# Twenty-four stores of routing blocks issued from SyncE's DMA queue where ScalarE's queue issued them

## The chip, the cores and the metric

The kernel runs on one core of a Trainium2 chip. The core has five engines that run their own instruction streams: TensorE (PE in the profile), VectorE (DVE), ScalarE (ACT), GpSimd (POOL) and SyncE (SP). ACT and SP can each issue DMAs, each on a queue of its own; SP does nothing else here. Data lie in HBM, in the on-chip memory SBUF, and in PSUM, into which PE writes. The metric is the device time of one execution in microseconds (us), as the median of several runs; lower is better.

## What is computed

A two-layer trunk over 512 tokens of 1024 features: an mLSTM mixer in the first layer, stick-breaking attention in the second, and after each a PEER feed-forward block. Only the PEER block matters here. For every token and each of 8 heads it picks 16 of 16384 experts by two lists of 128 keys, and sums those experts:

```python
s_top, i_top = lax.top_k(s, PEER_TOPK)                       # per head, two lists of 128 keys
cand = s_top[:, :, 0, :, None] + s_top[:, :, 1, None, :]     # 16 x 16 pairs
g_top, pos = lax.top_k(cand, PEER_TOPK)
expert = jnp.take_along_axis(cand_idx, pos, axis=-1)
g = jax.nn.softmax(g_top, axis=-1)
u = jnp.take(peer_u, expert, axis=0)
act = jax.nn.gelu(jnp.einsum('thkd,td->thk', u, xb))
vv = jnp.take(peer_v, expert, axis=0)
out = jnp.einsum('thk,thkd->td', g * act, vv)
```

## The kernel before

For 384 of the 512 tokens the kernel does not gather: it computes all 16384 activations as 128 dense blocks (`ua` or `pp`, 24 matmuls of 128x384 each), multiplies them by a dense matrix of routing weights that is zero where an expert was not picked, and multiplies the product with `peer_v` (`y`). The other 128 tokens are gathered, by GpSimd, later on.

`peer(l)` runs once in each layer. The part that the change touches is its **routing stage**, in which two things are woven together on the same engines:

- The routing weights are made in 48 chunks of 8 tokens. VectorE writes one-hot rows `oA`, `oB` (L1021, L1022), GpSimd scales them to `oH` (L1024), VectorE and ScalarE make the low-order part `oL` (L1028, L1033), PE multiplies them into `gps` (L1041, L1042), and ScalarE copies `gps` out of PSUM into the block `stg` (L1044, twice in a chunk). After every fourth chunk a block of 32 tokens is full and is stored to HBM, to `Gd` (L1046): 12 stores in each layer, 24 in all. `stg` has two buffers, `gps` two.
- Between the chunks stand 64 of the dense activation blocks (`early_acts`). For each, SyncE loads 512 KB of `peer_u` into `wraw` (L915, three buffers), ScalarE casts it to `whi` (L917), VectorE takes the remainder `wlo` (L925), which frees `wraw`, PE makes 24 matmuls (L936), and ScalarE applies Gelu (L942 or L945). From the 17th block on the result is stored to HBM as `spd` (L946), from ScalarE's queue, 48 times in each layer.

The order on PE, VectorE and ScalarE is the order in which this code is written (`manual_schedule`); SyncE's is set by a scheduler. On ScalarE a store of `spd` is followed by the cast of the load that is used two blocks later:

```python
nc.scalar.dma_start(spd[a // 4][:, (a % 4) * ND:(a % 4 + 1) * ND], ga)   # L946
```

After the routing stage the next one begins with loads `gb` of the stored weights (L1134, SyncE's queue), which wait until all 12 stores of the layer have landed, and goes on with the matmuls `y` (L1177) and the other 64 activation blocks `pp` (L1125).

Of the kernel before, what the change touches and what calls it, by code (L numbers as in the profile page):

```python
# [49 lines left out]
def body(tc, nc, A, ctx):  # L50
# [803 lines left out]
    def peer(l):  # L854
        U, Vw, Ur, Vr = A["u"][l], A["v"][l], A["u_rows"][l], A["v"][l].rearrange("a p d -> (a p) d")
        Gd = dram.tile([NGRP, 128, GROW], F32, name=f"g{l}")
        keep = KEEP[l]
        with ExitStack() as st:
# [19 lines left out]
            with ExitStack() as s1:  # L878
# [156 lines left out]
                def place(s, c, stg, oB, oA, oH, oL, gl, o):  # L1035

                    for j in range(CHUNK // 4):
                        gps = pq.tile([128, 4, 128], F32, name="gps", bufs=2)
                        for i in range(4):
                            n = 4 * j + i  # L1040
                            PE.matmul(gps[:, i], oB[:, n], oH[:, n], start=True, stop=False)  # L1041
                            PE.matmul(gps[:, i], oB[:, n], oL[:, n], start=False, stop=True)  # L1042
                        k = c * CHUNK + 4 * j
                        S.activation(stg[:, :, k:k + 4], gps.rearrange("p t a -> p a t"), AF.Copy, scale=1.0 / GSCALE)  # L1044
                    if c == 32 // CHUNK - 1:
                        nc.scalar.dma_start(Gd[:, :, s * 128:(s + 1) * 128].rearrange("g p c -> p g c"),  # L1046
                                            stg.rearrange("p (g a) t -> p g (a t)", a=4))

                late = None
# [8 lines left out]
                for t in range(NGT, 4):  # L1058
                    gen = routed(t + 1) if t < 3 else gathered()
                    for sub in range(4):  # L1060
                        stg = gp.tile([128, 128, 32], F32, name="stg")
                        for c in range(32 // CHUNK):
                            ones_of = expand(t, sub * 32 + c * CHUNK)
                            advance(gen, RCHUNK)
                            sofar += 1
                            ran += share()
                            if late:
                                place(*late)
                            scale(*ones_of)
                            sofar += 1  # L1070
                            ran += share()
                            late = ((t - NGT) * 4 + sub, c, stg, *ones_of)
                    advance(gen, 1e9)
                place(*late)
                run(24 * NPRE)

# [221 lines left out]
```

## Time and profile before

| | |
|---|---|
| median of 3 runs | 3242.69 us (3240.5 to 3249.38) |
| the profiled execution | 3245.62 us |
| its span in the profile | 3243.9 us |
| routing stage, first store to last, layer 0 | 554.4 to 823.2 us |
| routing stage, first store to last, layer 1 | 2171.7 to 2436.0 us |
| DMA bytes of ScalarE's queue | 69.29 MB in 112944 packets |
| DMA bytes of SyncE's queue | 451.75 MB in 119680 packets |

Times in the trace are counted from the start of the span. An engine's name with a q behind it (ACTq, SPq) is its instruction sequencer, which issues DMAs; such an instruction counts as no work of the engine, but the engine's next instruction waits for it. A wait "A <- B" says that A stood idle until B's last instruction was done.

### The profile page before, as it was taken

The page shows a single profiled execution, that of the slowest core. Times are in us where ns is not written, and L with a number is a line of the kernel's source. Part 1 is how long each engine was busy: PE and PEld are TensorE (multiplying, and loading weights), DVE is VectorE, ACT ScalarE, POOL GpSimd, SP SyncE. Part 2 cuts the span into 40 slices and gives each one's busy share as a digit, 9 for nine tenths or more (in the row PEclk, how much of TensorE's full clock was granted, in tenths as well). Part 3 has the DMA queues.
Part 4 walks back from the last instruction along what each step waited for, and adds up shares of the span by engine and source line. Part 5 has one row for each costly group of instructions (what it writes and reads, how often), then busy time and mean ns, then how long its engine had stood idle before and what let it go on. Part 6 is the DMA issues. An engine that isn't in the chain of part 4 may idle for free. (4 is left out here: it accounts for less than half of the span.)

```text
span 3243.9 us, 45180 instructions
## 1 busy us (share of the span) xinstructions
PE 3127.5 (96%) x16168; PEld 2660.2 (82%) x16168; DVE 2440.9 (75%) x4501; ACT 1351.9 (42%) x2133; POOL 1497.3 (46%) x1592
## 2 busy tenths in 40 slices
PE   7998999999999999999989999999999999999999
PEld 5746789988888888888867657898988888888887
DVE  5745479777688788888883584897776888888887
ACT  5344335556433333333342553356663333333332
POOL 0433523887344444444453454248883444443443
PEclk9979999999999999999989899999999999999999
DMA  6733224676899899999854102246779998999997
GB/s 249 258 123 118 79 72 143 208 237 208 321 354 342 328 362 336 343 352 330 314 190 142 39 7 80 73 144 213 235 219 331 342 354 329 355 347 337 356 331 273
DMA packets 306578, 792.40 MB, mean 244 GB/s; under 512 B 24368, under 2 KB 135216, under 8 KB 306352
## 3 DMA queue, kind: packets, MB, share of 16 engines
q1 hardware_dynamic: 119680, 451.75, 39.1%
q0 software_dynamic: 73728, 268.47, 22.7%
q10 hardware_dynamic: 112944, 69.29, 7.3%
q8 instruction: 126, 2.06, 0.3%
q14 instruction: 100, 0.82, 0.1%
HBM read 718.12 MB, written 71.30 MB: 243 GB/s over the span
## 5 line engine op out<-in xcount | busy, mean ns | idle before, releaser
L103 ACT CAST whi<-wraw 128x1024 fp32r<-128x1024 f32 x481 | 501.2, 1049 | 676.2 <-PE y L1177 245.0
L1024 POOL TENSOR_SCALAR oH<-oA,gh 128x128 f16<-128x128 f16 x768 | 467.0, 630 | 249.4 <-DVE oA L1021 212.6
L104 DVE TENSOR_TENSOR wlo<-wraw,whi 128x1024 fp32r<-128x1024 f32 x393 | 477.7, 1223 | 135.1 <-ACT whi L103 133.5
L1095 POOL DMA_INDIRECT rows<-in_u_rows,pidx x256 | 337.5, 1318 | 472.5 <-DVE rows L1102 415.0
L1095 POOL DMA_INDIRECT rows<-in_v,pidx x256 | 326.5, 1276 | 447.8 <-DVE yt L1113 403.9
L1177 PE MATMUL y<-wlo,Wh 128*128 128x512 f32 x1536 | 480.7, 391 | 0.0
L1177 PE MATMUL y<-whi,Wl 128*128 128x512 f32 x1536 | 472.6, 390 | 0.0
L1177 PE MATMUL y<-whi,Wh 128*128 128x512 f32 x1536 | 443.9, 392 | 7.5 <-ACT Wh L103 7.5
L104 POOL TENSOR_TENSOR wlo<-wraw,whi 128x1024 fp32r<-128x1024 f32 x88 | 221.5, 2519 | 377.9 <-ACT whi L103 377.9
L936 PE MATMUL ua<-hh,wlo 128*128 128x384 f32 x1024 | 348.2, 340 | 2.9 <-DVE wlo L925 2.9
L936 PE MATMUL ua<-hh,whi 128*128 128x384 f32 x1024 | 347.4, 339 | 1.4 <-ACT sf L895 1.4
L936 PE MATMUL ua<-hl,whi 128*128 128x384 f32 x1024 | 346.8, 339 | 0.0
L1125 PE MATMUL pp<-hh,wlo 128*128 128x384 f32 x1024 | 343.7, 336 | 0.2
L1125 PE MATMUL pp<-hl,whi 128*128 128x384 f32 x1024 | 343.7, 336 | 0.0
L1125 PE MATMUL pp<-hh,whi 128*128 128x384 f32 x1024 | 343.2, 335 | 0.0
L1177 PEld LDWEIGHTS y<-whi,Wh 128*128 128x128 f32 x1536 | 287.6, 188 | 62.1 <-ACT Wh L103 9.0
L1177 PEld LDWEIGHTS y<-wlo,Wh 128*128 128x128 f32 x1536 | 289.2, 188 | 59.4
L1177 PEld LDWEIGHTS y<-whi,Wl 128*128 128x128 f32 x1536 | 288.2, 188 | 59.5
L1113 DVE SCALAR_TENSOR_TENSOR yt<-rows,uw,yt 128x1024 f32<-128x1024 f32 x254 | 327.0, 1288 | 8.9 <-DMA rows<-in_v,pidx 6.6
L1102 DVE SCALAR_TENSOR_TENSOR rows<-rows,htok 128x1024 f32<-128x1024 f32 x256 | 308.9, 1219 | 13.5 <-DMA rows<-in_u_rows,pidx 13.4
L119 PE MATMUL pp<-hh,whi 128*128 128x512 f32 x560 | 223.7, 407 | 14.1 <-ACT hh L234 7.2
L119 PE MATMUL pp<-hl,whi 128*128 128x512 f32 x560 | 224.9, 402 | 0.0
(320 smaller groups left out, 5629.9 us busy)
## 6 DMA issues: line engine op xcount, KB each, us to landing
wraw<-in_u SPq DMA_DIRECT2D x256, 512.0 KB
wraw<-in_v SPq DMA_DIRECT2D x256, 512.0 KB
g<-stg ACTq DMA_DIRECT2D x24, 2048.0 KB
gb<-g SPq DMA_DIRECT2D x64, 768.0 KB
araw<-in_ada_w SPq DMA_DIRECT2D x80, 512.0 KB
spd<-ga ACTq DMA_DIRECT2D x96, 192.0 KB
ga<-spd SPq DMA_DIRECT2D x24, 768.0 KB
wraw<-in_peer_q SPq DMA_DIRECT2D x32, 512.0 KB
```

What stands on the lines that cost most here:

```text
L103: S.copy(hi, src)
L104: eng.tensor_tensor(lo, src, hi.bitcast(F32), op=OP.subtract)
L119: PE.matmul(ps, a[:, ws], b[k], start=k == 0 and i == 0, stop=k == KD - 1 and i == 2)
L936: PE.matmul(ps, p[:, ws], q[k][:, T0:T], start=n == 0, stop=n == 3 * KD - 1)
L1024: G.tensor_scalar(oH[:, n], oA[:, n], gh[:, o + n:o + n + 1], 1.0, op0=OP.mult, op1=OP.mult)
L1095: tc.keep_in_program_order(G.indirect_dma_start(out=r, out_offset=None, in_=rows, in_offset=bass.IndirectOffsetOnAxis(ap=pidx[:, n:n + 1], ...
L1102: V.scalar_tensor_tensor(r, r, 1.0, htok, op0=OP.mult, op1=OP.mult, accum_out=uw[:, n:n + 1])
L1113: V.scalar_tensor_tensor(yt, r, uw[:, n:n + 1], yt, op0=OP.mult, op1=OP.add)
L1125: PE.matmul(ps[:, :ND], p[:, ws], q[k][:, T0:T], start=n == 0, stop=n == 3 * KD - 1)
L1177: PE.matmul(y[t][d], wa[:, ts], vb[:, d * 512:(d + 1) * 512], start=n == 0 and i == 0, stop=n == NA - 1 and i == 2)
```

## The change

One line: the store of a full routing block is issued from SyncE's queue. What it copies, and when its data are ready, stay as they were.

```diff
                     if c == 32 // CHUNK - 1:
-                        nc.scalar.dma_start(Gd[:, :, s * 128:(s + 1) * 128].rearrange("g p c -> p g c"),
+                        nc.sync.dma_start(Gd[:, :, s * 128:(s + 1) * 128].rearrange("g p c -> p g c"),
                                             stg.rearrange("p (g a) t -> p g (a t)", a=4))
```

The order on PE, VectorE and GpSimd is the same row for row. On ScalarE, layer 0, around the second store, this stood before (`stg` the block, `gps` the product in PSUM, `ga` a Gelu result):

```order
L1044 ACTIVATE stg<-gps 128x128x4 x2
L1046 DMA g_2427<-stg 128x32x128
L1033 ACTIVATE oL<-oA,gl 128x128 x3
L945 ACTIVATE ga<-ua 128x384
L946 DMA spd_4_2441<-ga 128x384
L917 CAST whi<-wraw 128x1024
```

and of a later store, as a piece of the difference:

```order
 L917 CAST whi<-wraw 128x1024
 L1044 ACTIVATE stg<-gps 128x128x4 x2
-L1046 DMA g_2427<-stg 128x32x128
 L1033 ACTIVATE oL<-oA,gl 128x128 x3
 L945 ACTIVATE ga<-ua 128x384
```

The store has left ScalarE's stream, and nothing else there has moved. On SyncE, layer 0, the whole routing stage and the first loads behind it stood like this before:

```order
L108 DMA wraw<-in_peer_q 128x1024 x10
L915 DMA wraw<-in_u 128x1024 x64
L108 DMA wraw<-in_u 128x1024 x3
L108 DMA wraw<-in_v 128x1024
L108 DMA wraw<-in_u 128x1024
L108 DMA wraw<-in_v 128x1024 x2
L1134 DMA gb<-g_2427 128x1536 x2
```

Now the stores stand among the loads. SyncE, layer 0, the last three of the twelve:

```order
L915 DMA wraw<-in_u 128x1024 x3
L1046 DMA g_2427<-stg 128x32x128
L915 DMA wraw<-in_u 128x1024 x5
L108 DMA wraw<-in_u 128x1024
L1046 DMA g_2427<-stg 128x32x128
L108 DMA wraw<-in_u 128x1024 x2
L108 DMA wraw<-in_v 128x1024
L108 DMA wraw<-in_u 128x1024
L108 DMA wraw<-in_v 128x1024
L1046 DMA g_2427<-stg 128x32x128
L108 DMA wraw<-in_v 128x1024
L1134 DMA gb<-g_2427 128x1536 x2
```

Ahead of the first store stand 20 loads of `peer_u`, and between one store and the next 3 to 6 loads; in layer 1 the same numbers return. Each load behind a store is issued after it.

## Rows read from the trace of the kernel before

**Rows 1.** The page: busy us, share of the span and instructions of each engine

```profile
PE 3127.5 (96%) x16168; PEld 2660.2 (82%) x16168; DVE 2440.9 (75%) x4501; ACT 1351.9 (42%) x2133; POOL 1497.3 (46%) x1592
```

**Rows 2.** DMA issues by line, layer 0: minimum/median/maximum ns, first and last start us

```profile
L946 ACTq DMA_DIRECT2D spd<-ga x48: 326/327/7011, 559.4 to 821.1; - x48
...
L1046 ACTq DMA_DIRECT2D g<-stg x12: 377/377/394, 554.4 to 823.2; - x12
...
L915 SPq DMA_DIRECT2D wraw<-in_u x49: 327/328/340, 530.0 to 790.3; - x49
```

**Rows 3.** ScalarE's longest wait, total us, times, longest; layer 0, then layer 1

```profile
ACT whi L917 <- issue: 49.6, 10, 7.1
...
ACT whi L917 <- issue: 47.9, 10, 6.6
```

**Rows 4.** Whom PE waited for, first to last store of layer 0: us, times, longest

```profile
PE gps L1041 <- ACT stg L1044: 6.3, 7, 1.5
PE gps L1042 <- ACT oL L1033: 5.2, 8, 1.1
```

**Rows 5.** The same of layer 1

```profile
PE gps L1042 <- ACT oL L1033: 5.5, 9, 1.1
PE gps L1041 <- ACT stg L1044: 3.6, 5, 1.1
```

**Rows 6.** The same, 2360 to 2370 us, where ScalarE changes its function table

```profile
PE gps L1042 <- ACT oL L1033: 1.1, 1, 1.1
PE gps L1041 <- ACT stg L1044: 1.1, 1, 1.1
```

**Rows 7.** The same behind the tenth stores: layer 0, then layer 1

```profile
PE gps L1041 <- ACT stg L1044: 0.9, 1, 0.9
...
PE gps L1042 <- ACT oL L1033: 0.5, 1, 0.5
...
PE gps L1041 <- ACT stg L1044: 0.6, 1, 0.6
```

**Rows 8.** In order of time (start, us, instruction [idle before]): layer 0's tenth store, SyncE's next loads

```profile
771.66 0.39 ACTq L1046 DMA_DIRECT2D g<-stg  x1
...
771.75 1.56 SPq L915 DMA_DIRECT2D wraw<-in_u  x2
...
773.50 7.01 ACTq L946 DMA_DIRECT2D spd<-ga  x1
780.55 1.05 ACT L917 CAST whi<-wraw 128x1024 fp32r<-128x1024 f32 x1 [7.08 <-issue]
...
784.23 1.05 ACT L917 CAST whi<-wraw 128x1024 fp32r<-128x1024 f32 x1 [0.40 <-ACT ga L945]
```

**Rows 9.** In order of time: a load on SyncE and its cast, no store near

```profile
2103.48 0.33 SPq L915 DMA_DIRECT2D wraw<-in_u  x1
...
2108.26 1.05 ACT L917 CAST whi<-wraw 128x1024 fp32r<-128x1024 f32 x1 [0.17 <-DMA wraw<-in_u]
```

**Rows 10.** In order of time: loads after layer 0's first store, casts behind stores one and two

```profile
557.38 1.57 SPq L915 DMA_DIRECT2D wraw<-in_u  x2
...
564.57 1.06 ACT L917 CAST whi<-wraw 128x1024 fp32r<-128x1024 f32 x1 [0.47 <-DMA wraw<-in_u]
567.41 1.09 ACT L1044 ACTIVATE stg<-gps 128x512 f32<-128x512 f32 x2 [1.79 <-PE gps L1042]
...
574.77 0.38 ACTq L1046 DMA_DIRECT2D g<-stg  x1
...
586.05 0.49 ACT L945 ACTIVATE ga<-ua 128x384 f32<-128x384 f32 x1 [0.84 <-PE ua L936]
```

**Rows 11.** The chain that ended last, in order of time: end of layer 1's routing stage

```profile
2436.05 11.73 DMA g<-stg
```

**Rows 12.** PE in order of time: two products that follow each other without a wait

```profile
2434.40 0.22 PE L1041 MATMUL gps<-oH,oB 128*128 128x128 f16 x1
2434.45 0.22 PE L1042 MATMUL gps<-oL,oB 128*128 128x128 f16 x1
```

## The prediction

> **What bounds the kernel now.** The page comes first: PE is busy for 96% of the span [rows 1]. So what can be won lies where PE has gaps, and the view to read next is that of the issues by line, on the queue that the change relieves. The store of `spd` at L946 takes 0.33 us to issue as a rule but up to 7.0 us [rows 2]. In order of time the long ones stand right behind a routing store: at 771.66 the store is issued, at 773.50 the next issue on the same queue begins and lasts 7.01 us, and the cast that follows in ScalarE's stream stands idle for 7.08 us [rows 8]. ScalarE loses 49.6 us in ten such waits in layer 0 and 47.9 us in ten in layer 1 [rows 3], 4.9 us each. The trace shows so much: an issue behind one of these stores (4096 runs of 512 bytes, by the code) is held up for 4 to 7 us.
>
> What matters is what PE loses by it. Between the first and the last store PE waits for ScalarE's `stg` copies and `oL` parts for 6.3 + 5.2 = 11.5 us in layer 0 and 5.5 + 3.6 = 9.1 us in layer 1 [rows 4, 5]: 20.6 us in 29 waits, against 97.5 us that ScalarE stands. Most of the stalls are covered, since ScalarE catches up before PE needs it.
>
> **What the change removes.** ScalarE's stream loses 24 issues of 0.377 us [rows 2] and, if the stall goes with the store, the twenty waits. Not all of PE's 20.6 us are owed to the stall. At four places ScalarE changes its function table for the `exp` of the routing; one of them costs PE 1.1 + 1.1 us [rows 6], the four 2.2, 2.2, 1.5 and 1.5, together 7.4 us in 8 waits. Behind each layer's first store, where no stall follows, PE waits 0.5 us once; that leaves 20.6 - 7.4 - 1.0 = 12.2 us in 19 waits. The two tenth stores hold 0.9 + 0.5 and 0.6 + 0.5 = 2.5 us of it in 4 waits [rows 7], which I expect to stay (next part): 9.7 us in 15 waits go. Each wait costs PE somewhat more than the view says: a product of `gps` shows 0.22 us but the next begins 0.05 us later [rows 12], so a break loses about 0.16 us besides. 15 x 0.16 = 2.4 us, and the term is 12.1 us.
>
> **What it adds.** SyncE's stream gets 24 issues; the store is then ahead of the loads on SyncE's queue. Three things can cost there.
>
> First, SyncE may wait for a full `stg` with loads behind it. By the order and the trace it hardly does: the load that now stands behind the store was issued later than the store already, as its buffer came free only then: 3.0 us later at the first store (554.4 and 557.38) [rows 2, 10], and 0.1 us at the tenth, the closest of layer 0 [rows 8]. I put this at nothing; who would wait is the cast of that load.
>
> Second, the issue of the next load is held up as that of `spd` is now, and its data come behind the store's. The trace has no load behind a store on one queue, so I bound its landing, counted from the store's issue. Below: in layer 0 a load issued at 557.38, 3.0 us after the first store but on the other queue, let its cast go at 564.57, 10.2 us after the store [rows 10]. Above: the store takes 11.7 us from its issue to the first instruction that waited for it [rows 11], and an undisturbed load takes 4.8 us from issue to cast [rows 9]: 16.5 us if the load began only when the store is done. Between them, as the issue comes free 5.7 to 8.9 us after the store (8.85 at the tenth, rows 8), the load would land 4.5 us later, at 10.2 to 13.3 us; I take 12, as `spd`'s held issue is the nearest row. When is it wanted? ScalarE casts two earlier loads first. Behind the second store the third cast follows a Gelu that starts 11.3 us after the store and itself waited for PE [rows 10], so removing the stall does not move it: it is wanted at 12.2 us, and I take this for ten stores of each layer, at no cost. At the first stores it is wanted at 10.2 us, 1.8 us too soon; ScalarE's next copy idles 1.79 us for PE there [rows 10], so most is covered: 0.5 us each, bounds 0 and 1.8. At the tenth store the load behind it is the second cast. Blocks follow each other every 5.4 us (49 loads in 260 us, rows 2), so without a stall that cast is wanted about 7.4 us after the store and gets its data at 12; now it stands at 784.23, 12.6 us after the store [rows 8]. A stall of ScalarE's queue is swapped for a wait for a load, with PE's 2.5 us unchanged.
>
> Third, the last store of each layer, on which the next stage waits, 11.7 us [rows 11]. It keeps its place in time; between 1 us sooner (no loads of the other queue between its packets) and 1 us later I take nothing.
>
> **The sum.** 12.1 - 2 x 0.5 = 11.1 us off the profiled execution's 3245.6 us gives 3234.5 us. That execution lies 2.9 us above the median of the runs shown, so the forecast is 3242.7 - 11.1 = 3231.6 us, 0.34% less. What a measurement of this kernel can tell from no change is about 0.3%, 9.7 us: the line stands at 3233.0 us, close by.
>
> **The rivals.** *No change: the loads hold ScalarE where its queue did.* If a load lands at the upper bound of 16.5 us, a cast wanted at 12.2 us waits 4.3 us at nearly every store, against 4.9 us now; PE gets back 0.6/4.9 of the 12.1 us, 1.5 us: 3241 us. For it speaks that the store and the load now share a queue; against it, that 10.2 us and the held issue bring the landing nearer to 12. The Trainium skill has another reason for the same outcome: "DMA: Bandwidth & Descriptors", section "Issuing engines are not separate DMA queues", says that DMAs of all issuing engines share the same 16 engines and that issuing from several saves only the sequencer's time, usually small beside the transfer. By that rule the sum would be nothing, 3242.7 us; the trace does not agree as far as the time of the issue goes, up to 7.0 us instead of 0.33 [rows 2].
>
> *Slower: ScalarE is held as before, and the loads come late besides.* This is so if an issue on one queue has to wait while the other queue's store is being issued. Then ScalarE loses its 4.9 us per store and up to 4.3 us more for the load; if PE's loss grows in proportion it nearly doubles, 12.2 us and 19 x 0.16 = 3.0 us: 15 us more, 3258 us. It is decided by one thing, whether `spd`'s issue stays long with the store on the other queue. The mirror image is in the trace: in layer 0 SyncE issued 49 loads while ScalarE's queue carried the stores, one at 557.38, 3.0 us after a store, and none took over 0.34 us [rows 2, 10]. That speaks clearly against it. [...]
>
> *Faster than forecast.* With ScalarE 5 us ahead the waits at the table changes and the tenth stores may shrink too. The most there is to win is all 29 waits: 20.6 + 29 x 0.16 = 25.2 us, 3217 us.
>
> **How the numbers follow.** My forecast, 0.57, with 0.44 below 3233.0 us and 0.13 above it, as the gain is close to the line and its terms are good to some 5 us; no change, 0.25; slower, 0.09, of which 0.01 would still be within 0.3%; faster than forecast, 0.09. So faster by over 0.3% has 0.44 + 0.09 = 0.53, within it 0.13 + 0.25 + 0.01 = 0.39, slower 0.08. The range goes from 3217 us, the most there is to win, to 3247 us, the no-change case with a load or two still later and the spread of the runs; it leaves out the slower rival and little else.
>
> **What would show it.** In the profile after, no issue at L946 should last over about 0.4 us, and the wait of `whi` for the queue should be gone; if it stays, the slower rival holds. Some load at L915 behind each store should take 4 to 8 us to issue. Casts at L917 should wait for `wraw` at the first and tenth stores, by 2 and 4 us; if they wait at nearly every store, it is the no-change case. PE's waits for `stg` and `oL` in the stage should fall from 20.6 us to about 11 us, and each layer's last store should come 5 to 6 us sooner after its first. A store that SyncE reaches well before `stg` is full, with loads waiting behind it, would make the prediction wrong in a way that I put at nothing.

## The result, and the profile after

The changed kernel takes 3199.87 us (median of 4 runs, 3193.14 to 3208.78), the kernel before beside it 3245.29 us: a ratio of 0.988, with a 95% interval of 0.985 to 0.991. The forecast was 3231.6 us with a range from 3217 to 3247 us. The direction was right; the gain is about four times as large as foretold, and the time lies below the range. The profiled execution takes 3194.85 us, its span is 3193.1 us, 50.8 us less than before.

Where those 50.8 us are, by the first and last store of each layer: at the first store of layer 0 the changed kernel is 1.5 us ahead (552.9 for 554.4), at the last 21.0 us (802.2 for 823.2), at the first of layer 1 34.4 us (2137.3 for 2171.7), at the last 49.2 us (2386.8 for 2436.0), at the end 50.8 us. So the two routing stages gave 19.5 and 14.8 us, 34.3 us in all, and the part between them 13.4 us. The stages are the change's doing; the part between is taken up below.

The page's first part, the counterpart of [rows 1], has PE at 97%: 32.8 us less busy for the same instructions.

```profile
PE 3094.7 (97%) x16168; PEld 2645.3 (83%) x16168; DVE 2437.3 (76%) x4501; ACT 1355.2 (42%) x2133; POOL 1510.2 (47%) x1592
```

The issues by line (minimum, median and maximum in ns; first and last start in us), both layers for L946 and for the stores, layer 0 for the loads at L915, the counterparts of [rows 2]:

```profile
L946 ACTq DMA_DIRECT2D spd<-ga x96: 326/326/336, 557.3 to 2384.7; - x96
...
L1046 SPq DMA_DIRECT2D g<-stg x24: 377/377/387, 552.9 to 2386.8; - x24
...
L915 SPq DMA_DIRECT2D wraw<-in_u x44: 327/328/4917, 555.8 to 774.1; - x44
```

The long issues have left `spd` and gone to the loads behind a store. SyncE now stands in front of each store until the block is full. Its waits in layer 0's stage (us, times, longest), and the eleventh store with the load behind it (start, us):

```profile
SPq L1046 <- ACT oL L1033: 31.9, 11, 4.5
...
SPq L1046 <- ACT stg L1044: 0.8, 1, 0.8
```

```profile
781.19 0.38 SPq L1046 DMA_DIRECT2D g<-stg  x1
781.83 6.75 SPq L108 DMA_DIRECT2D wraw<-in_u  x1
```

(The view names `oL`, the instruction behind the copy; each of these waits ended within 0.03 us of the end of the last copy into `stg`.) No load is late by these 32.7 us: in both layers the buffer of the load behind a store comes free only after the store is issued, 0.6 us after it at the closest, which is the eleventh.

The waits of layer 0's stage (us, times, longest), where [rows 3, 4] have `whi` standing 49.6 us for the queue and PE 11.5 us for `stg` and `oL`:

```profile
ACT stg L1044 <- PE gps L1042: 30.7, 30, 1.9
...
DVE wlo L925 <- ACT whi L917: 12.2, 7, 2.8
ACT whi L917 <- DMA wraw<-in_u: 7.7, 5, 3.5
...
PE gps L1041 <- POOL oH L1024: 2.7, 6, 0.8
ACT whi L103 <- DMA wraw<-in_u: 2.2, 1, 2.2
```

PE's matmuls wait for ScalarE nowhere; only its six short waits for GpSimd are left. ScalarE now waits for PE. Casts do wait for their loads, 7.7 + 2.2 us, but PE does not notice. Layer 1 reads the same, with 7.0 + 1.8 us for the casts and 2.1 us of PE for GpSimd.

Each stage in one row (length in us, busy us and instructions of PE, PEld, DVE, ACT and POOL, granted clock, DMA share, GB/s), first before, then after:

```profile
554.40:823.20 268.80, 253.96 (x1865) 240.78 (x1864) 207.64 (x432) 162.00 (x324) 210.40 (x342) 0.99 0.71 218
2171.70:2436.00 264.30, 252.50 (x1865) 239.26 (x1864) 207.51 (x432) 161.87 (x325) 214.78 (x342) 0.99 0.73 222
```

```profile
552.90:802.20 249.30, 246.20 (x1864) 236.88 (x1863) 207.04 (x432) 163.45 (x324) 219.36 (x342) 1.00 0.76 235
2137.30:2386.80 249.50, 246.97 (x1872) 238.00 (x1871) 206.87 (x432) 163.76 (x324) 219.53 (x342) 1.00 0.76 235
```

PE's idle time in the two stages (length less busy) was 14.8 + 11.8 = 26.6 us and is 3.1 + 2.5 = 5.6 us: 21.0 us, close to the 20.6 us of waits of [rows 4, 5]. Its busy time for the same work fell too, by 7.8 + 5.5 = 13.3 us. The gain of 34.3 us is these two numbers, and the second is one that the list of PE's waits does not have.

### The profile page after: what moved, and what is told of

Same layout as the page of the kernel before. It is cut to its first block, busy times and chain, and to the rows that moved or that the text cites. A ratio compares the mean times of both kernels' runs of the same rounds, so it can differ in the third digit from the quotient of the medians.

```text
span 3193.1 us, 45198 instructions
## 1 busy us (share of the span) xinstructions
PE 3094.7 (97%) x16168; PEld 2645.3 (83%) x16168; DVE 2437.3 (76%) x4501; ACT 1355.2 (42%) x2133; POOL 1510.2 (47%) x1592
## 5 line engine op out<-in xcount | busy, mean ns | idle before, releaser
L1024 POOL TENSOR_SCALAR oH<-oA,gh 128x128 f16<-128x128 f16 x768 | 480.7, 648 | 205.5 <-DVE oA L1021 200.5
```

The costliest lines, as they stand in the source:

```text
L1024: G.tensor_scalar(oH[:, n], oA[:, n], gh[:, o + n:o + n + 1], 1.0, op0=OP.mult, op1=OP.mult)
```

## The experiments

**What the theories were.** After the result the question was how PE can win more than ScalarE's late copies cost it. *Theory A:* a stall that lies ahead of a change of ScalarE's function table comes back round VectorE. The rows of ScalarE in the kernel before, behind layer 0's fourth store:

```profile
622.08 0.38 ACTq L1046 DMA_DIRECT2D g<-stg  x1
...
623.89 5.80 ACTq L946 DMA_DIRECT2D spd<-ga  x1
629.74 1.05 ACT L917 CAST whi<-wraw 128x1024 fp32r<-128x1024 f32 x1 [5.88 <-issue]
...
642.07 1.28 ACT L777 ACT_TABLE_LOAD   x1
646.76 0.31 ACT L777 ACTIVATE eg<-eg 128x128 f32<-128x128 f32 x1 [3.40 <-DVE eg L775]
647.09 1.28 ACT L945 ACT_TABLE_LOAD   x1
```

and VectorE's in the same stretch:

```profile
626.12 0.24 DVE L757 FIND_INDEX8 px<-gt,cd 128x8 uint32<-128x84 f32 x1
630.82 1.23 DVE L925 TENSOR_TENSOR wlo<-wraw,whi 128x1024 fp32r<-128x1024 f32 x1 [4.46 <-ACT whi L917]
...
646.44 0.28 DVE L775 TENSOR_TENSOR eg<-gt 128x128 f32<-128x128 f32 x1
```

The held issue delays the cast; VectorE, in order, stands 4.46 us for the cast at `wlo` (L925), and all its further work comes later, the input `eg` of the routing's `exp` among it (L775). ScalarE has caught up meanwhile, arrives at the `exp` (L777) too early, and stands again, 3.40 us, in front of a second table load. One stall has stopped ScalarE twice. After the change ScalarE finds its input ready:

```profile
638.62 1.28 ACT L777 ACT_TABLE_LOAD   x1
639.94 0.31 ACT L777 ACTIVATE eg<-eg 128x128 f32<-128x128 f32 x1
640.27 1.28 ACT L945 ACT_TABLE_LOAD   x1
```

There are two such places in each layer, behind the fourth and the eighth store, and before, ScalarE lost 7.0 us in each layer there. Of the waits of layer 0's stage before, this one and, for later, that of the `stg` copies for PE:

```profile
ACT stg L1044 <- PE gps L1042: 17.7, 19, 1.9
...
ACT eg L777 <- DVE eg L775: 7.0, 2, 3.6
```

*Theory B:* every store costs PE about the same, and the table changes are as dear without the stalls. The rival causes of the gain itself were the store's place (which queue carries it) and chance (where the granted clock fell in the attention).

**The kernel before once more.** No edit.

> The kernel before, unchanged, profiled once more. Question: of the 50.8 us between the two profiled executions, 34.3 lie in the two routing stages and about 14.5 elsewhere, 11.5 of it in the attention layer around 1816 to 1847 us, where the trace of before shows 30.7 us at half the granted clock and the trace after shows none. Theory A (chance of one execution): the routing stages repeat at 268.8 and 264.3 us within 1 us, while the half-clock stretch at 1816 us is of another length or absent, and the span differs by up to 12 us. Theory B (belongs to the kernel before): the stretch returns with 30 us, and the span is 3243.9 us within 2.

3239.6 us, stages of 266.4 and 264.1 us, waits for `eg` of 5.5 us in layer 0 and 7.0 us in layer 1. Neither theory came out as put: the half-clock stretch returned at its full 30.7 us, but the span was 6.0 us shorter (3237.9 us), 2.4 us of it in layer 0's stage. The stages' lengths belong to the kernel, to within 2.4 us here and 4.7 us in a later run.

**Two stores of each layer, those ahead of a table change.**

```diff
-                        nc.scalar.dma_start(Gd[...
+                        (nc.sync if s in (3, 7) else nc.scalar).dma_start(Gd[...
```

> Only the fourth and the eighth store of each layer go to SyncE's queue, the other twenty stay on ScalarE's. They are the stores ahead of the two function-table changes in each stage. Theory A (the stall comes back through VectorE): ScalarE's stall at these two makes its casts late, VectorE waits for the casts, the routing's exp input comes late, ScalarE waits for it 3.5 us twice in a layer, and PE waits at the table changes. Then PE's waits at the table changes (7.4 us in both layers) go with these four stores, beside their own waits (1.2 + 1.2 and 1.4 + 0.5): the stages shrink by some 8 to 10 us in layer 0 and 7 to 8 in layer 1, the time by 14 to 18 us, and ScalarE's wait for eg (L777, 7.0 us in each stage) is gone. Theory B (as predicted: the table changes cost by themselves): only the own waits go, 4.3 us and their breaks, 5 us in all.

Measured: 3221.7 us, ratio 0.994 [0.992, 0.996]; stages of 258.2 and 257.9 us. Layer 0's waits:

```profile
ACT whi L917 <- issue: 36.9, 8, 7.7
...
ACT eg L777 <- DVE eg L775: 0.8, 1, 0.8
```

Four stores of 24 gave 10.6 + 6.4 = 17.0 us, half of the 34.3 us, though eight of ten waits for the queue stayed. (Counted from the second profile of before it is 14.4 us.) The wait for `eg` went from 7.0 to 0.8 us.

**Two other stores of each layer, the ones next to them.**

```diff
-                        nc.scalar.dma_start(Gd[...
+                        (nc.sync if s in (4, 8) else nc.scalar).dma_start(Gd[...
```

> The counterpart: only the fifth and the ninth store of each layer, those right behind the table changes, go to SyncE's queue. Theory A (the stall comes back through VectorE from the store before): the waits at the table changes stay at 7.4 us and ScalarE's wait for eg at 7.0 us in each stage; only the waits behind these stores go (1.5 and 1.1 + 0.5, and the later GpSimd waits of 0.6 and 0.4): 4 to 6 us. Theory B: the same 5 us, and no difference from the run with the fourth and eighth.

Measured: 3238.75 us, ratio 0.999 [0.997, 1.001]; stages of 267.6 and 264.0 us, 1.2 and 0.3 us shorter. Layer 0's waits:

```profile
ACT eg L777 <- DVE eg L775: 7.0, 2, 3.6
ACT whi L917 <- DMA wraw<-in_u: 4.6, 3, 2.6
```

The same number of stores moved, the same number of waits for the queue gone (eight are left in either layer), and hardly any gain: 1.5 us in the stages and 2.9 us in the medians, where theory A had 4 to 6. The wait for `eg` is whole. Theory B falls, theory A holds.

Nor is it the length of a stall that makes it dear. The tenth stores hold `spd` longest, 7.0 and 6.6 us, and with the change the stretch from there to the next store got only 1.8 and 0.5 us shorter. The stretches behind the fourth and eighth stores, with stalls of 5.8 to 6.7 us, got 4.7 to 5.5 us shorter each, 20.8 of the 34.3 us.

**The mirror image: all moved but the fourth and eighth.** An edit of the changed kernel.

```diff
-                        nc.sync.dma_start(Gd[...
+                        (nc.scalar if s in (3, 7) else nc.sync).dma_start(Gd[...
```

> The change, but the fourth and the eighth store of each layer stay on ScalarE's queue (the mirror image of the kernel that moved these four alone, which took 10.5 and 6.4 us off the two stages). If each store has a price of its own, as my sum had it, what those four gave back is missing here: the stages take about 260 and 256 us. If ScalarE is only late at these places because the stalls of the stores before have used up its lead, the four stalls of 4 to 7 us are still there but mostly covered: no or hardly any wait for eg, and stages of 249.5 to 253 us.

Measured: stages of 258.5 and 258.5 us (one execution, 3225.9 us). Waits and windows of layer 0:

```profile
ACT whi L917 <- issue: 11.0, 2, 6.4
...
ACT eg L777 <- DVE eg L775: 7.0, 2, 3.6
```

```profile
554.80:813.30 258.50, 250.81 (x1865) 238.93 (x1864) 207.28 (x432) 162.84 (x324) 217.65 (x342) 0.99 0.73 227
```

The four stores cost 9.2 + 9.0 = 18.2 us even when no stall goes before them; my second case, that they would then be covered, is refuted. Each costs about 4.5 us, where its stall of ScalarE lasts 5.5. The other twenty cost the remaining 16 us, 0.8 us each. Of the 9.2 us in layer 0, PE's idle time holds 7.7 - 3.1 = 4.6 us and its busy time 250.81 - 246.20 = 4.6 us.

**The stalled issue moved in place of the store.** `spd` is stored from SyncE's queue, the routing blocks stay with ScalarE's.

```diff
-                                        nc.scalar.dma_start(spd[a // 4][...
+                                        nc.sync.dma_start(spd[a // 4][...
```

> The routing stores stay on ScalarE's queue, and the 96 stores of spd (L946) go to SyncE's instead, so that ScalarE issues nothing behind a routing store. Theory A (what cost was ScalarE's instruction stream held at the issue behind the store): the wait of whi for the issue is gone and the stages come to about 250 us each, as in the changed kernel, 30 to 45 us off the time, unless SyncE, which now waits for each Gelu, brings loads too late. Theory B (what gains is the store itself on SyncE's queue, sooner or with less in its way): no gain, stages of 265 to 269 us.

Measured: 3208.73 us, ratio 0.991 [0.989, 0.993]; stages of 249.4 and 249.8 us. The issues at L946, both layers, and PE's waits in layer 0:

```profile
L946 SPq DMA_DIRECT2D spd<-ga x96: 319/326/1172, 557.9 to 2395.0; - x96
```

```profile
PE gps L1041 <- POOL oH L1024: 2.0, 5, 0.8
PE gps L1042 <- ACT oL L1033: 0.5, 1, 0.5
```

The stages are as short as with the change, with every store where it was. Which queue the store is on matters only through what is issued behind it on ScalarE's. (SyncE's issues are not quite untouched here: up to 1.17 us behind a store of ScalarE's.)

**What the hold-up goes by.** The routing weights lie in HBM block by block, so that a store of the same 2 MB writes 128 runs of 16 KB in place of 4096 of 512 bytes; it stays on ScalarE's queue.

```diff
-        Gd = dram.tile([NGRP, 128, GROW], F32, name=f"g{l}")
+        Gd = dram.tile([NSUB, 128, NGRP * 128], F32, name=f"g{l}")
...
-                        nc.scalar.dma_start(Gd[:, :, s * 128:(s + 1) * 128].rearrange("g p c -> p g c"),
-                                            stg.rearrange("p (g a) t -> p g (a t)", a=4))
+                        nc.scalar.dma_start(Gd[s], stg.rearrange("p a t -> p (a t)"))
...
-                    nc.sync.dma_start(gbs[g].rearrange("p s a t -> p (s a t)"), Gd[g, :, 0:NSUB * 128])
+                    nc.sync.dma_start(gbs[g].rearrange("p s a t -> p s (a t)"),
+                                      Gd[:, :, g * 128:(g + 1) * 128].rearrange("s p c -> p s c"))
```

> The stores stay on ScalarE's queue, but the routing weights lie in HBM block by block, so that a store of the same 2 MB is 128 runs of 16 KB in place of 4096 runs of 512 bytes (the loads behind the stage pay for it with runs of 512 bytes). If what holds the next issue is the making of many small packets, the issues of spd behind a store take 0.33 us, ScalarE's wait for its queue is gone and both stages take about 250 us. If it goes by the bytes of the store, spd still takes 4 to 7 us behind a store, the wait stays near 49 us in a layer and the stages near 264 to 269 us. The whole time says little here, as the loads and the order behind the stage change with it.

Measured: both stages 250.0 us; one execution of 3219.2 us, in which the loads behind the stage, now in short runs, and a changed order there are included. Issues at L946, both layers, and the packets of ScalarE's queue (112944 before):

```profile
L946 ACTq DMA_DIRECT2D spd<-ga x96: 326/326/361, 559.7 to 2403.9; - x96
```

```profile
q10 hardware_dynamic: 17712, 69.29, 5.8%
```

The same bytes on the same queue, and no issue is held. The hold-up goes by the runs into which the bytes are cut, not by the bytes; whether by the number of runs or by their shortness this pair can't tell.

**Layer 0 alone.**

```diff
-                        nc.scalar.dma_start(Gd[...
+                        (nc.sync if l == 0 else nc.scalar).dma_start(Gd[...
```

> The routing stores of layer 0 are issued from SyncE's queue, those of layer 1 from ScalarE's. If the gain is made in the routing stage and stays there, the first layer's stage (first store to last) takes about 249.5 us, as with the whole change, the second's about 264 us, as before; the longest waits of ScalarE for its queue are 0 in the first and some 47 us in the second; and the time falls by about 18 us plus or minus the 5 us that executions differ. If most of the measured gain came from elsewhere (a chance of where PE's clock stood), the time falls by much less than half, or by nearly all of it, though only one stage is shorter.

Measured: 3224.12 us, ratio 0.995 [0.993, 0.997], 17.6 us less than the 3241.70 us of before; stages of 249.7 and 268.8 us. Issues at L946 in layer 1, where nothing is changed:

```profile
L946 ACTq DMA_DIRECT2D spd<-ga x48: 326/326/7156, 2156.8 to 2418.5; - x48
```

Layer 1's stage, though unchanged, took 4.5 us more than in the first profile of before; it holds two half-clock stretches of 3.4 us, where that one has one. A layer's gain is made in its own stage and stays: between the stages it is 1347.3 us, as before.

**Both kinds of stores on SyncE's queue.** The change, and L946 from SyncE too.

> The routing stores and those of spd all on SyncE's queue, none on ScalarE's. If ScalarE's stream is all that mattered, the stages take about 249 us as with the change and the time is within 0.3% of it, about 3200 to 3208 us. If stores that wait for a Gelu hold up the loads behind them on the one queue, casts wait for wraw at nearly every store, PE waits for it by 10 to 20 us in a layer, and the time lies between the change and the kernel before, 3215 to 3235 us.

3206.12 us, ratio 0.990 [0.987, 0.993]; stages of 248.8 us both. No better than the change alone: with PE busy for 246 of 249 us only some 3 us of idle time are left in a stage. On SyncE, L946 takes up to 6.0 us behind a store, and it costs nothing there.

**The changed kernel again, and one more execution of it.** No edit.

> The changed kernel once more. If the gain is what the two stages show, 34 us, with 2 us at the boundary behind each of them, the stages take 249 us again, and the median lies 34 to 38 us below that of the kernel before run beside it; the first measurement's 45 us then had some 10 us from where the long half-clock stretch in the attention fell. Executions may differ by 10 us either way, as those of the kernel before do, with that stretch or without it. If the whole 45 us is owed to the change, the difference comes out at 43 to 47 us again and no profile of it shows the long stretch.

> The changed kernel once more, one profile. Both kernels' executions fall in two groups by time, about 10 us apart (before near 3234 and 3244 us, after near 3197 and 3207 us, each with the lower mean clock in the longer group). If the long half-clock stretch in the attention is what makes the groups, then an execution near 3207 us has it and one near 3197 us has not, with stages of 249 to 250 us either way; if the change is what removes the stretch, no execution of this kernel has it whatever its time.

The first: 3200.51 us, ratio 0.989 [0.986, 0.991], 41.2 us below before, between what the two cases had; stages of 249.3 and 250.5 us. The second: one execution of 3202.9 us, near neither of the two times expected; stages of 249.2 us both. The question was the part between the stages, 13.4 us shorter in the first pair of profiles. It holds a stretch of attention in which PE may run at half clock, and its windows (columns as above) show it before, not in the first profile after (the same matmuls, 22 us earlier and 12 us shorter), and again, not as long, in the second run:

```profile
1816.00:1846.70 30.70, 30.40 (x68) 12.99 (x66) 19.47 (x47) 15.83 (x34) 15.95 (x33) 0.50 0.06 18
```

```profile
1793.60:1812.60 19.00, 17.91 (x71) 8.62 (x70) 17.14 (x45) 15.07 (x35) 16.96 (x32) 1.00 0.09 29
```

```profile
1794.00:1814.50 20.50, 20.21 (x43) 8.50 (x43) 14.03 (x37) 12.16 (x28) 12.79 (x25) 0.51 0.07 26
```

The attention's 416 matmuls at L690, L712 and L729 take 122.2, 110.7 and 117.4 us in these three, from the first to the last: 11.5 of the 13.4 us. From the last store of layer 0 to the first of layer 1, profiles without the stretch take 1335.1 and 1336.4 us (the changed kernel) and 1335.0 us (the kernel with stores five and nine moved, whose stages are as long as before); profiles with it 1341.6 us (the second run), 1347.4 and 1348.5 us (before); the profiles of the other six edited kernels all have it, at 1345.0 to 1351.3 us. So the stretch comes and goes in kernels of either kind and is not what the change removes. The spread goes with it: of 34 executions of before timed beside the experiments 15 lie at 3226 to 3236 us and 19 at 3240 to 3251 us, of ten of the changed kernel six at 3193 to 3202 us and four at 3204 to 3209 us, the longer ones with the lower mean clock each time (the second run, with its shorter stretch, falls between). Group against group, by medians, the changed kernel is 37 us faster (3197.3 for 3234.3) and 38 us (3207.0 for 3244.7). I take 37 us as the change's own, an estimate, and the rest of the measured 41 to 45 us as a matter of how many executions of each group were among the runs; why the stretch comes in one execution and not in the next stays open.

## Why the prediction was wrong, step by step

The forecast took 11.1 us off: 9.7 us of waits, 2.4 us for the breaks they make, less 1.0 us. The stages gave 21.0 us of idle time and 13.3 us of busy time. So of the 23 us that are missing from the sum some 12 are waits that it let stay or added, and some 11 are the price of a break.

**Right: what the change does to the queues.** L946 is at 0.33 us throughout, the wait of `whi` for the queue is gone, loads behind a store take up to 4.9 us to issue (one at L108 6.7 us), and SyncE's waits for a full `stg` make no load late. The slower rival needed `spd` to go on waiting. SyncE's and ScalarE's rows of the changed kernel behind layer 0's first store:

```profile
552.88 0.39 SPq L1046 DMA_DIRECT2D g<-stg  x1
...
555.83 2.90 SPq L915 DMA_DIRECT2D wraw<-in_u  x1
...
557.29 0.34 ACTq L946 DMA_DIRECT2D spd<-ga  x1
```

While SyncE's load is held behind the store, an issue of ScalarE's goes through in 0.34 us. In both layers 17 of ScalarE's issues fall into such a time, and none takes longer.

**Right in the number, by luck in part: when the held load lands.** I took 12 us from the store's issue. The cast of that load starts 11.8 us after the first store and 11.6 us after the tenth. But my 12 us stood for an issue that comes free 7.5 us after the store and a load that then takes 4.5 us, as an undisturbed one does. At the first store the issue came free after 5.9 us (at 558.73), and the data took another 5.9 us. ScalarE:

```profile
564.64 1.05 ACT L917 CAST whi<-wraw 128x1024 fp32r<-128x1024 f32 x1 [2.67 <-DMA wraw<-in_u]
...
768.05 1.05 ACT L917 CAST whi<-wraw 128x1024 fp32r<-128x1024 f32 x1 [3.48 <-DMA wraw<-in_u]
```

**Wrong: what such a wait costs PE.** I charged 2.5 us for the tenth stores and 1.0 us for the first. ScalarE does wait there, 2.7 and 3.5 us in layer 0, and at four casts more than I named there, but PE waits for ScalarE at none of them. I compared a wait for a load (4 us) with a stall of the queue (7 us) and left PE's loss unchanged, where I should have asked how far ScalarE is ahead once nothing else holds it: its waits for PE at `stg` in layer 0 have grown from 17.7 to 30.7 us, and that lead covers the loads.

**Wrong, and the costliest step: "not all of PE's 20.6 us are owed to the stall".** I subtracted 7.4 us at the four table changes because a table change is there in either kernel. The rows in front of it would have told otherwise: ScalarE's wait for `eg` stood in the waits of before, 7.0 us in each stage, and what released it was a VectorE that had stood for ScalarE's own cast. [rows 6] showed whom PE waited for and when, and I put the cause down to the nearest event on that engine instead of following it back. The runs with four stores moved, and with all but these moved, price these stores at 17 to 18 us, half of what the stages gave.

**Wrong: the price of a broken-off PE, and so the cap.** The 0.16 us that I added for each wait was for the end of the last product only, and the most there is to win came out at 25.2 us. The stages gave 34.3: 21.0 us of idle time and 13.3 us of busy time, where 29 x 0.16 us make 4.6 us. A part of the rest is the clock. Windows of 4 us in the kernel before, ahead of and behind a place where PE broke off:

```profile
735.00:739.00 4.00, 4.00 (x35) 3.84 (x34) 3.88 (x12) 3.21 (x6) 1.74 (x5) 1.00 0.46 138
...
747.00:751.00 4.00, 1.80 (x12) 1.37 (x10) 3.83 (x12) 3.14 (x7) 4.00 (x9) 1.00 0.56 178
751.00:755.00 4.00, 4.00 (x24) 3.79 (x24) 3.93 (x9) 0.91 (x3) 3.30 (x5) 0.57 0.99 285
```

PE is busy throughout the first and the last, but in the last at a granted clock of 0.57 (mostly the lower level, 1.2 GHz). It begins 16 products of `gps` in the first and 15 in the last, and besides them 17 matmuls of a block in the first and 9 in the last: 8 fewer, at 0.17 us each, are 1.4 us lost that appear as work. PE's idle time stood ahead of it: between 747 and 751 us it was busy for 1.8 us of 4. The stages of before have three such stretches of 3.4 us (near 751, 809 and 2369 us), those of the first profile after none; the second has one, at 2167.6 us, right behind waits of PE for GpSimd. That is 4 to 5 us, an estimate; the remaining 4 us of the 13.3 I could not tell apart.

**Mis-sized: the last store.** Taken at nothing, with 1 us either way. In layer 1 it lands in 10.09 us where [rows 11] have 11.73, and the first `gb` behind it takes 5.92 us where it took 6.43: 2.2 us sooner together. The chain that ended last, before and after:

```profile
2448.30 6.43 DMA gb<-g
```

```profile
2386.80 10.09 DMA g<-stg
...
2397.42 5.92 DMA gb<-g
```

**The rule that spoke against the change.** By the Trainium skill, "DMA: Bandwidth & Descriptors", section "Issuing engines are not separate DMA queues", another issuing engine saves only the sequencer's time, usually small. The saving is of that kind, and the runs bear out that nothing else was won: with the stores in place and `spd` moved the stages are as short. But small it is not: twenty held issues of 3.5 to 7.0 us on an engine that PE waits for are worth some 37 us here.

## What to carry to other kernels

Keep stores of many short runs off the queue of an engine that computes, or give such a store long runs: what was issued soon behind it stood for microseconds here, and the engine with it. When a stall is priced, follow what it delays through the other in-order engines until it comes back, since one late cast made VectorE late and VectorE stopped ScalarE a second time; a cause is found by asking what released each wait in turn. PE's listed waits are a lower bound of what its breaks cost (21 of 34 us here): compare the length of the whole stage with the work in it.

## What the runs showed of the hardware

- Behind a 2 MB store of 4096 runs of 512 bytes the next issue on the same queue was held until 5.7 to 8.9 us after the store's issue (kernels before and after): for up to 7.0 us on ScalarE's queue, 7.7 us in the run with four stores moved, and for up to 6.7 us on SyncE's. Behind a store of the same bytes in 128 runs of 16 KB no issue of `spd` took over 0.36 us. In the kernels before and after, issues on the other queue within 5.7 us of a store took at most 0.34 us; with `spd` on SyncE and the stores on ScalarE's queue some took up to 1.17 us.
- PE's granted clock can fall to half for 3.4 us right behind a break of PE's work, at a price of about 1.4 us that shows as busy time. In the attention a stretch of 20 to 31 us at half clock comes in some executions of a kernel and not in others, worth 6 to 13 us.
